# One stream of products with the values per pair of heads, single banks for their sums, and part of the result sums in retention

## The chip, the cores and the metric

The kernel runs on one core of a Trainium2 chip. The metric is the time of one execution on the device in microseconds (us): the median of several runs.

## The reference

The block takes x of 1024 positions by 1024 channels in float32. A modulated RMS norm gives h, and one projection of h gives the inputs of two token mixers that run side by side: retention with 4 heads, in chunks of 128 positions, and dilated sliding-window attention with three groups of 4 heads (window 128 with dilation 1, 512 with 4, 2048 with 16). Each group has its own softmax; the three are merged by their log denominators:

```python
for gi, (win, dil) in enumerate(ATT_GROUPS):
    o, lse = dilated_group(heads(aq), heads(ak), heads(av), tab, win, dil)   # softmax(q k + bias) v in the window
    outs.append(o); lses.append(lse)
wts = softmax(stack(lses, axis=0), axis=0)
att = einsum('gbhs,gbhsd->bshd', wts, stack(outs, axis=0)).reshape(B, S, ATT_GROUP_W)
att_out = att @ w_att_out
merged = sigmoid(gate_a) * ret_out + sigmoid(gate_b) * att_out
return merged @ w_o
```

A residual sum, a second norm, an MLP with a squared ReLU and a final norm follow. They are not touched here.

## The kernel before

Everything is float32, computed as three products of a high and a low part each (`mm3`, lines 200, 202 and 204: low weight by high input, high by low, high by high). The parts are made by a cast on ScalarE and a subtraction on VectorE.

The work is a list of steps (`Steps`, line 54). A step is one projection of h (`proj_gen`, which yields after each block of six matmuls) with other work woven between its matmuls. Weights come from DRAM into a ring of three raw tiles, and are split into their two parts ahead of the step that uses them: for an ordinary step before its body runs, for a step marked `manual` when its body calls `ahead`. Instructions are issued to each engine's queue in the order in which the Python code runs, and each engine works its queue in order; a tile's buffer is used again when its last reader is done.

PSUM has eight banks of 512 float32 columns. From the attention on they are dealt as two tiles of two banks (`ps_mm`, tag "mm", for projections and for the sums over the values) and four single banks (`ps_s`, tag "s", for scores and transpositions).

Retention (`chunk`, line 731) runs 4 heads of 8 chunks one after the other, and is called once per chunk. GpSimd has two operations in each chunk: `gr` (line 809), a power that VectorE needs for `nb` (line 715), and the subtraction `j` (line 639), the low part of q and k for a later chunk. Retention's output y goes to DRAM in four quadrants. `result_sums` (line 593), called at the start of attention, makes four sums of quadrants from DRAM to DRAM: eight DMAs of 2 MB on GpSimd's queue, four copies and four that add to their target. They are read much later as the inputs of the product with the output weights.

Attention runs in two pairs of heads; a pair has six combinations of group g and head a, in the order g = 1, 2, 0 (`combos`). Steps ak0 to ak5 project the keys and weave the scores in; `scores_end` leaves the probabilities in tiles P. `weights` (line 1571) turns the softmax statistics into the merging weights, which go through DRAM to be laid out for groups 1 and 2, and `pscale` (line 1600) multiplies the probabilities by them, half on VectorE (line 1605) and half on ScalarE (line 1607). Then come gate steps (`cover_step`), projections whose result goes through a sigmoid (line 1777) straight out of PSUM and to DRAM (line 1778). The products with the values are woven between their matmuls. In the first pair they are gate00 (n=0, with the last scores), gate01 (n=1), gate02 (n=2, with the products of group 0) and gate03 (n=3, group 1); group 2's products lie in ak0 of the second pair, named ak10. The second pair has gate04, gate05 and gate06 (group 0), and `gate_step` (gate9, groups 1 and 2).

One item of the products is a bank of up to four 128x128 transpositions of P (`pv_tr`, line 1622), a cast into the high part (`pth`, line 1626), a subtraction for the low part (`ptl`, line 1627), and later the products (`pv_mm`, lines 1646 to 1648) that add to a sum of 1024 columns in a two-bank tile. A pair has 20 items: four for each head of groups 0 and 1, two for each of group 2. Products run three items behind the transpositions; the queue of items is filled at the beginning of each call of `pv` and drained at its end. `pv_end` takes a finished sum out of PSUM into P of group 0: a copy for group 0 (line 1655), additions for groups 1 and 2 (line 1659), and at the end the split into `ah` and `al` (lines 1664, 1665). The values come by `v_fetch` (line 1529) and are split in `v_split` (lines 1539, 1540).

Of the kernel before, what the change touches and what calls it, by code (L numbers as in the profile page):

```python
# [11 lines left out]
F32 = mybir.dt.float32  # L12
# [5 lines left out]
P = 128  # L18
# [115 lines left out]
def block_kernel(ctx, tc, io, stop=None, dbg=None):  # L134
# [12 lines left out]
    def banks(single):  # L147

        if PS:
            PS["ctx"].close()  # L150
        PS["i"] = PS.get("i", 0) + 1
        PS["ctx"] = ExitStack()
        PS["p"] = PS["ctx"].enter_context(tc.tile_pool(name=f"psum{PS['i']}", bufs=2, space=bass.MemoryType.PSUM,
                                                       reuse_waits="tile"))
        PS["n"] = 8 if single else 4

    banks(True)

    def ps_mm(name):
        return PS["p"].tile([P, 2, 512], F32, tag="mm", bufs=2, name=name)  # L160

    def ps_s(name, shape=(P, 512)):
        return PS["p"].tile(list(shape), F32, tag="s", bufs=PS["n"], name=name)

# [416 lines left out]

    def dma_sum(out, x, y):

        flat = lambda t: t.rearrange("p a b -> p (a b)").rearrange("p (a b) -> p a b", b=2048)
        nc.gpsimd.dma_start(flat(out), flat(x))
        nc.gpsimd.dma_start(flat(out), flat(y), accum_op=ALU.add, max_dma_last_dim=8192)

# [4 lines left out]

    def result_sums():
        b11, b12, b21, b22 = (y_d[:, i] for i in range(4))
        dma_sum(yt_d["t1"], b11, b12)
        dma_sum(yt_d["t3"], b12, b22)
        dma_sum(yt_d["t2"], yt_d["t1"], b22)
        dma_sum(yt_d["t4"], yt_d["t2"], b21)

# [131 lines left out]
    def chunk(h, c, ahead, w=None):  # L731
# [6 lines left out]
        if g == 2:  # L738
            first["release"]()
        if w:  # L740
            hd["w"] = w
# [620 lines left out]

    A = {}
    att_ctx = ExitStack()
# [169 lines left out]

    def v_split(pair, g):
        for j in range(2):
            lo = A["l", g, j]
            hi = v_tile(pair, g, j, "vh")
            nc.scalar.copy(hi, fv(lo))
            nc.vector.tensor_sub(lo, fv(lo), fv(hi))  # L1540
            A["v", g, j] = (hi, lo)

# [20 lines left out]
    def stats_out(pair, g):  # L1563

        if g == 1:
            A["stn"] = A["p"].tile([P, 3, 8, 4], F32, tag="stn", name=f"stn{pair}")
        d = dram.tile([S, 4], F32, name=f"std{pair}{g}")
        nc.sync.dma_start(natural(d, g, 4), blocks(A["st"][:, g], g))
        nc.sync.dma_start(A["stn"][:, g], natural(d, 0, 4))

    def weights(pair):
# [10 lines left out]
        for g in range(3):  # L1582
            nc.vector.tensor_sub(wt[:, g], stn[g][:, :, 0:2], mx)
        nc.scalar.activation(wt, wt, AF.Exp)
        for g in range(3):
            nc.vector.tensor_mul(pr[:, g], wt[:, g], stn[g][:, :, 2:4])
# [9 lines left out]
        for g in (1, 2):  # L1596
            nc.sync.dma_start(blocks(wg[:, g - 1], g), natural(ds[g - 1], g, 2))
            A["w", g] = wg[:, g - 1]

    def pscale(g, a):  # L1600
        t, w = A["P", g, a], A["w", g]
        for blk in range(8):
            v = pslice(g, t, blk)[0]
            if blk in (0, 2, 4, 5, 7):
                nc.vector.tensor_scalar_mul(v, v, w[:, blk, a:a + 1])
            else:
                nc.scalar.mul(v, v, w[:, blk, a:a + 1])
        A["scaled", g, a] = True

# [19 lines left out]

    def pv_mm(g, a, bank, pt, acc, seen):  # L1630
        ph, pl = pt
# [7 lines left out]
        for i, q, k, n in runs:  # L1639
            cs = slice(i * 128, (i + n) * 128)  # L1640
            bk = q // 4
            o = acc[:, bk, (q % 4) * 128:(q % 4 + n) * 128]
            v = (vblk(g, k, a, 0), vblk(g, k, a, 1))
            first = bk not in seen
            seen.add(bk)
            nc.tensor.matmul(o, v[1], ph[:, cs], start=first, stop=False, skip_group_check=True)
            nc.tensor.matmul(o, v[0], pl[:, cs], start=False, stop=False, skip_group_check=True)
            nc.tensor.matmul(o, v[0], ph[:, cs], start=False, stop=True, skip_group_check=True)

    def pv_end(pair, g, a, acc):  # L1650

        f = flat(acc)
        sumt = A["P", 0, a][:, :1024]
        if g == 0:
            nc.scalar.copy(sumt, f)
        else:
            r = 4 * g
            sv = sumt.rearrange("p (i r) -> p r i", r=r)
            nc.vector.tensor_add(sv, f.rearrange("p (r i) -> p r i", r=r), sv)
        if g == 2:  # L1660
            h = 2 * pair + a
# [5 lines left out]

    def pv(pair, *groups):


        items = [(g, a, bank) for g in groups for a in range(2) for bank in PT[g]]
        accs = {}
        queue = []

        def mm(g, a, bank, pt):
            if (g, a) not in accs:
                accs[g, a] = (ps_mm(f"pv{pair}{g}{a}"), set())
            pv_mm(g, a, bank, pt, *accs[g, a])
            if bank is PT[g][-1]:
                pv_end(pair, g, a, accs[g, a][0])  # L1680
                return True
            return False

        for item in items:
            if item[2] is PT[item[0]][0]:
                del A["scaled", item[0], item[1]]
            queue.append((*item, pv_tr(pair, *item)))
            yield item is items[2]
            if len(queue) == 3:
                yield mm(*queue.pop(0))  # L1690
        for item in queue:
            yield mm(*item)

    def weave_pv(main, n, pair, *groups):


        parts, waits = sum(4 * len(PT[g]) for g in groups), 2 * len(groups) + 1
        heavy = max(1.0, (parts - waits) / max(1, n - waits))
        total = parts + waits * (heavy - 1)
        done = share = 0  # L1700
        for wait in pv(pair, *groups):
            share += heavy if wait else 1
            while done * total < share * n:
                next(main, None)
                done += 1
        drain(main)

    combos = [(g, a) for g in (1, 2, 0) for a in range(2)]

    def att_step(pair, i):  # L1710
# [3 lines left out]
        def body(*args):  # L1714
            ps = ps_mm(f"ak{pair}{i}")
            gen = proj_gen(ps, hd.pop("w") if i == pair == 0 else args[-1])
            if i == len(combos) - 1:
                v_fetch(pair, 0)
# [3 lines left out]
            elif pair == 0:  # L1722
# [6 lines left out]
                u_final(H - 1)  # L1729
                result_sums()  # L1730
                open_att()
                args[0](3)
            else:

                weave_pv(at(gen, 0, lambda: v_split(0, 2)), NK - 1, 0, 2)
# [3 lines left out]
            k_split(pair, g, a, ps)  # L1739
            if i > 0:  # L1740
# [5 lines left out]
    def cover_step(pair, n):  # L1746


        i = COVER[pair][n]

        def body(*args):
            ps = ps_mm(f"gate0{i}")
            gen = proj_gen(ps, args[-1])
            if n == 0:
                v_fetch(pair, 1)
                weave(gen, 6, scores_gen(pair, *combos[-1]), len(SB[0]), lag=2, rest=False)
                drain(gen)
                scores_end(pair, *combos[-1])
                weights(pair)
                for a in range(2):  # L1760
                    pscale(0, a)
            elif n == 1:
                drain(at(gen, 4, lambda: v_split(pair, 0)))
            elif n == 2:
                v_fetch(pair, 2)

                gen = at(gen, 3, lambda: (args[0](3), v_split(pair, 1)))
                weave_pv(gen, NK - 1, pair, 0)
                for a in range(2):
                    pscale(1, a)  # L1770
            else:
                weave_pv(at(gen, 3, lambda: [pscale(2, a) for a in range(2)]), NK - 1, pair, 1)
            if n > 1:
                t = A["r1"].tile([P, S], F32, tag="att", bufs=8, name=f"g0{i}s")
            else:
                t = ring(f"g0{i}s", F32)
            nc.scalar.activation(t, flat(ps), AF.Sigmoid)
            nc.sync.dma_start(gate_d[i], t)
        return body

    for pair in range(2):
        for i, (g, a) in enumerate(combos):
            steps.add(att_step(pair, i),
                      ([] if i == pair == 0 else [wsplit(io["w_ak"][g * 4 + 2 * pair + a])]) +
                      ([(aq_d[pair, *combos[i - 1]], q_prep(pair, *combos[i - 1]))] if i > 0 else []),
                      manual=i == pair == 0)
        for n in range(len(COVER[pair])):
            more = [(aq_d[pair, *combos[-1]], q_prep(pair, *combos[-1]))] if n == 0 else []
            steps.add(cover_step(pair, n), more + [wsplit(io["w_gate"][len(COVER[0]) * pair + n])], manual=n == 2)

# [4 lines left out]

    def gate_step(w):

        ps = ps_mm("gate9")
        gen = at(proj_gen(ps, w), 2, lambda: v_split(1, 2))
        gen = at(gen, 3, lambda: [pscale(2, a) for a in range(2)])  # L1800
        weave_pv(gen, NK - 1, 1, 1, 2)
        att_ctx.close()
# [12 lines left out]

    steps.add(gate_step, [wsplit(io["w_gate"][len(COVER[0] + COVER[1])])])

# [885 lines left out]
```

## Time and profile before

| | before |
|---|---|
| median of 3 runs | 2194.77 us (2193.68 to 2197.47) |
| the profiled execution's own time | 2196.09 us |
| its span in the trace | 2194.1 us |
| TensorE busy | 2151.7 us (98%) |
| VectorE busy | 1472.7 us (67%) |
| ScalarE busy | 944.5 us (43%) |
| GpSimd busy | 166.4 us (8%) |
| mean granted TensorE clock | 0.998 |

Engines are named PE (TensorE matmul), PEld (its weight loads), DVE (VectorE), ACT (ScalarE), POOL (GpSimd) and SP (the queue that issues most DMAs). A row of waits names the waiting engine, tile and line, then what it waited for and where that is written, then the total, the count and the longest in us. A row of a timeline has start and length in us, engine, line, operation, written and read tiles, and in brackets the idle time before it with its releaser. A row of groups has busy us and mean ns behind the bar, then the idle time before it. A tile's view has the minimum, median and maximum length in ns. The end of a matmul is modelled.

### The profile page before, as it was taken

The numbers are of one execution on the slowest core, as the hardware profiler recorded it, in microseconds if no ns is written. First come the engines' busy times: TensorE is split into PE (matmuls) and PEld (weight loads), VectorE is DVE, ScalarE is ACT, GpSimd is POOL, SyncE is SP. The second block draws the span as 40 slices with busy tenths as digits, with TensorE's granted clock in tenths as the row PEclk, the third lists the DMA queues.
The fourth block names the chain that finished last, engine by engine and source line by source line (L and its number), as shares of the span: only waits on it lengthen the run. The fifth ranks groups of instructions, "written<-read, shape, count | busy, mean of one in ns | idle before, by whom it ended". The sixth has DMA issues, their size and how long they took to land.

```text
span 2194.1 us, 26997 instructions
## 1 busy us (share of the span) xinstructions
PE 2151.7 (98%) x10034; PEld 1784.1 (81%) x10034; DVE 1472.7 (67%) x2271; ACT 944.5 (43%) x1709; POOL 166.4 (8%) x176
## 2 busy tenths in 40 slices
PE   7999999999999999999999999999999999999998
PEld 5888888888888888888788788888878888788887
DVE  6756777767566677755555644777876665787855
ACT  4532322333334566654544524434454544533412
POOL 0101111100001233200000000001000000000003
PEclk9999999999999999999999999999999999999999
DMA  9869999734687745579523364654154435645322
GB/s 382 227 199 293 289 308 279 222 130 149 244 294 291 250 159 192 173 239 258 151 78 107 106 240 170 234 187 139 44 206 149 152 137 193 243 135 175 113 86 78
DMA packets 159906, 422.54 MB, mean 193 GB/s; under 512 B 27478, under 2 KB 55389, under 8 KB 155358
## 3 DMA queue, kind: packets, MB, share of 16 engines
q1 hardware_dynamic: 151902, 372.57, 48.2%
q0 software_dynamic: 7872, 48.24, 9.5%
q8 instruction: 79, 1.29, 0.2%
q14 instruction: 53, 0.43, 0.1%
HBM read 325.71 MB, written 160.32 MB: 222 GB/s over the span
## 4 chain that ended last, share of the span: by engine, by line
PE 84%; DVE 7%; ACT 4%; DMA 3%; issue 1%; SPq 0%; POOL 0%; POOLq 0%; DVEq 0%; ACTq 0%
PE qap L200 6%; PE qap L204 6%; PE qap L202 6%; PE fp L200 4%; PE fp L202 4%; PE fp L204 4%; PE f2a L202 2%; PE f2a L204 2%; PE f2a L200 2%; PE ak L200 1%; PE ak L202 1%; PE ak L204 1%; PE rg L202 1%; PE rg L200 1%; PE rg L204 1%; PE va L204 1%
## 5 line engine op out<-in xcount | busy, mean ns | idle before, releaser
L200 PE MATMUL qap<-hh,qaw 128*128 128x512 f32 x264 | 102.9, 390 | 0.5 <-DVE qat L291 0.5
L204 PE MATMUL qap<-hh,qaw 128*128 128x512 f32 x264 | 102.7, 389 | 0.0
L202 PE MATMUL qap<-hl,qaw 128*128 128x512 f32 x264 | 102.7, 389 | 0.0
L639 POOL TENSOR_TENSOR j<-qk,j 128x512 fp32r<-128x512 f32 x32 | 48.1, 1506 | 324.1 <-ACT j L638 324.1
L2158 ACT ACTIVATE a<-a 128x512 f32<-128x512 f32 x48 | 30.3, 632 | 78.2 <-DVE a L2157 78.2
L2054 POOL TENSOR_TENSOR accnf<-accnf,sqnf 128x256 f32<-128x256 f32 (+1 forms) x18 | 16.6, 922 | 612.4 <-ACT sqnf L2053 612.4
L1510 ACT ACTIVATE P<-P,ng 128x128 f32<-128x128 f32 (+1 forms) x96 | 41.9, 438 | 43.9 <-DVE ng L1507 43.9
L200 PEld LDWEIGHTS qap<-hh,qaw 128*128 128x128 f32 x264 | 49.5, 188 | 11.5 <-DVE qat L291 1.4
L204 PEld LDWEIGHTS qap<-hh,qaw 128*128 128x128 f32 x264 | 49.6, 188 | 10.3
L202 PEld LDWEIGHTS qap<-hl,qaw 128*128 128x128 f32 x264 | 49.5, 188 | 10.3
L2347 ACT CAST w2h<-w2s 128x512 fp32r<-128x512 f32 x36 | 22.4, 621 | 78.4 <-DVE w2s L2385 78.4
L257 DVE TENSOR_TENSOR fw<-w1r,fw 128x512 fp32r<-128x512 f32 x48 | 32.8, 688 | 33.3 <-ACT fw L247 33.3
L257 DVE TENSOR_TENSOR qaw<-wa,qaw 128x512 fp32r<-128x512 f32 x66 | 45.0, 686 | 12.7 <-ACT qaw L247 12.6
L2054 POOL TENSOR_TENSOR accn<-accn,sqn 128x512 f32<-128x512 f32 x12 | 15.5, 1295 | 477.2 <-ACT sqn L2053 477.2
L247 ACT CAST qaw<-wa 128x512 fp32r<-128x512 f32 x66 | 39.8, 617 | 25.5 <-PE qap L204 15.3
L200 PE MATMUL fp<-h2h,fw 128*128 128x512 f32 x128 | 50.0, 391 | 0.0
L204 PE MATMUL fp<-h2h,fw 128*128 128x512 f32 x128 | 49.8, 389 | 0.0
L202 PE MATMUL fp<-h2l,fw 128*128 128x512 f32 x128 | 49.8, 389 | 0.0
L200 PE MATMUL roa<-rh,rwl 128*128 128x512 f32 x128 | 49.8, 389 | 0.0
L202 PE MATMUL roa<-rl,rwh 128*128 128x512 f32 x128 | 49.8, 389 | 0.0
L204 PE MATMUL roa<-rh,rwh 128*128 128x512 f32 x128 | 49.8, 389 | 0.0
L1288 DVE SCALAR_TENSOR_TENSOR cossin<-cossin,cb 128x1024 f32<-128x1024 f32 x32 | 39.0, 1219 | 15.9 <-DMA cossin<-in_w_ada_dram 15.9
(3057 smaller groups left out, 7106.1 us busy)
## 6 DMA issues: line engine op xcount, KB each, us to landing
cossin<-in_w_ada_dram SPq DMA_DIRECT2D x32, 512.0 KB, 5.4
v<-vd SPq DMA_DIRECT2D x32, 512.0 KB, 4.7
w1r<-in_w_ff_dram SPq DMA_DIRECT2D x32, 512.0 KB, 4.9
vd<-vo SPq DMA_DIRECT2D x24, 512.0 KB, 6.6
yt<-y POOLq DMA_DIRECT2D x6, 2048.0 KB, 15.3
xsd<-as SPq DMA_DIRECT2D x24, 512.0 KB, 3.0
w2r<-in_w_ff2s_dram SPq DMA_DIRECT2D x24, 512.0 KB, 7.4
em<-in_w_ada_dram SPq DMA_DIRECT2D x16, 512.0 KB, 10.2
```

The source lines that it names most:

```text
L200: nc.tensor.matmul(o, wl, xh, start=first, stop=False, skip_group_check=skip)
L202: nc.tensor.matmul(o, wh, xl, start=False, stop=False, skip_group_check=skip)
L204: nc.tensor.matmul(o, wh, xh, start=False, stop=last, skip_group_check=skip)
L247: nc.scalar.copy(t[:, :512], src)
L257: nc.vector.tensor_sub(t[:, 512:], src, fv(t[:, :512]))
L639: nc.gpsimd.tensor_sub(t[:, 1], src, fv(t[:, 0]))
L1288: nc.vector.scalar_tensor_tensor(t, t, 1.0, cb, op0=ALU.mult, op1=ALU.mult, accum_out=mods[:, j:j + 1])
L1510: nc.scalar.activation(v, v, AF.Exp, bias=ng[:, blk:blk + 1], accum_out=st[:, g, blk, 2 + a:3 + a])
L2054: (nc.vector if f == 7 else nc.gpsimd).tensor_add(G["acc", key], G["acc", key], sq)
L2158: nc.scalar.activation(o, o, AF.Relu)
L2347: nc.scalar.copy(hi, src)
```

## The change

1. The products with the values of a pair become one generator, `pv_stream`, of 40 parts (20 transposition items, 20 products). `weave_pv` runs a given number of parts in each step: 16 in gate02, 14 in gate03 and 10 in ak10 for the first pair, 20 in gate06 and 20 in gate9 for the second. A projection's first block comes after the first three parts of a pair, or after the first two in a later step. `pscale` of a head comes two items before its first transposition.
2. While a stream runs, PSUM is dealt anew (`banks_pv`): one two-bank tile for projections, two single banks for transpositions, and four single banks for the sums, one for each head and half. `pv_end` works by halves of 512 columns.
3. Gate n=0 is copied out of PSUM by ScalarE and gate n=1 by VectorE at the end of their steps; their sigmoids run at parts 3 and 5 of the stream (`gate_out`).
4. The values' split is divided: for group 0 the casts are made in step n=0 and the subtractions inside `weights`; for groups 1 and 2 they are made at parts 12, 15, 24 and 27 (`pv_calls`). The fetch for group 0 comes one step earlier.
5. The reads of statistics and merging weights from DRAM are put off to `later_loads`, and the steps with streams, with n=1 and the first of the second pair are manual, calling `ahead` at named parts.
6. The result sums of retention's heads 0 and 1 are made by 16 DMAs of 512 KB, one issued at the start of each chunk from the last of head 1 on. The eight at the start of attention, for heads 2 and 3, are of 1 MB.

```diff
+    def ps_ac(name, j):
+        tag = f"ac{j % 4}"
+        return PS["first"].pop(tag, None) or PS["p"].tile([P, 512], F32, tag=tag, bufs=1, name=name)
+    def banks_pv(order):
+        banks(False)
+        PS["n"], PS["mm"] = 2, 1
+        for t in order:
+            PS["first"][t] = ps_mm("mmf") if t == "mm" else ps_s("sf") if t == "s" else ps_ac(t + "f", int(t[2]))
...
+        if c == 7 and h in (1, 2):
+            hd["sums"] = result_sums(slice(2 * h - 2, 2 * h))
+        if hd.get("sums"):
+            hd["sums"].pop(0)()
...
-    def pv_end(pair, g, a, acc):
-        f = flat(acc)
+    def pv_end(pair, g, a, acc, hf):
         sumt = A["P", 0, a][:, :1024]
         if g == 0:
-            nc.scalar.copy(sumt, f)
+            nc.scalar.copy(sumt[:, 512 * hf:512 * hf + 512], acc)
         else:
-            r = 4 * g
-            sv = sumt.rearrange("p (i r) -> p r i", r=r)
-            nc.vector.tensor_add(sv, f.rearrange("p (r i) -> p r i", r=r), sv)
+            n = 2 * g
+            sv = sumt.rearrange("p (i r) -> p r i", r=2 * n)[:, n * hf:n * hf + n]
+            nc.vector.tensor_add(sv, acc.rearrange("p (r i) -> p r i", r=n), sv)
...
+        for k, (g, a, i) in enumerate(PV):
+            if k + 2 < len(PV) and PV[k + 2][2] == 0:
+                pscale(*PV[k + 2][:2])
+            queue.append((g, a, i, pv_tr(pair, g, a, PT[g][i])))
+            yield
             if len(queue) == 3:
-                yield mm(*queue.pop(0))
+                mm(*queue.pop(0))
+                yield
...
+    def weave_pv(main, n, pair, parts, ahead, last=None):
+        lead = 2 if first == 0 else 1
+        for y in range(parts):
+            next(A["pv", pair])
+            while done < n and done * (parts - lead - 1) <= (y - lead) * n:
                 next(main, None)
                 done += 1
+            for call in calls.get(first + y, ()):
+                call()
+    def pv_calls(pair):
+        calls = {1: [later_loads], 3: [lambda: gate_out(pair, 0)], 5: [lambda: gate_out(pair, 1)]}
+        for g, y in ((1, 12), (2, 24)):
+            for j in range(2):
+                calls[y + 3 * j] = [lambda g=g, j=j: v_split(pair, g, j)]
+        for y in (9, 20, 35) if pair == 0 else (9, 22):
+            calls[y] = [lambda: calls["ahead"](3)]
...
             if n == 0:
+                later_loads()
+                for j in range(2):
+                    vs_high(pair, 0, j)
+                t = ring(f"g0{i}s", F32)
+                nc.scalar.copy(t, flat(ps))
+                A["gate", 0] = t, t
                 scores_end(pair, *combos[-1])
                 weights(pair)
-                for a in range(2):
-                    pscale(0, a)
+                pscale(0, 0)
             elif n == 1:
-                drain(at(gen, 4, lambda: v_split(pair, 0)))
+                drain(gen)
+                t = ring(f"g0{i}s", F32)
+                nc.vector.tensor_copy(t, flat(ps))
+                A["gate", 1] = t, t
-            nc.scalar.activation(t, flat(ps), AF.Sigmoid)
-            nc.sync.dma_start(gate_d[i], t)
```

More of the change, by code (lines that the diff above doesn't have):

```diff
@@ L1628, in pv_tr, with pv_mm @@
         return ph, pl
-    def pv_mm(g, a, bank, pt, acc, seen):
+    def pv_mm(pair, g, a, bank, pt, accs):
         ph, pl = pt
@@ L1689, in pv @@
             if len(queue) == 3:
-                yield mm(*queue.pop(0))
+                mm(*queue.pop(0))
+                yield
         for item in queue:
[L1692 to L1703, printed above, removed]
+            mm(*item)
```

152 lines of the change are left out of this document (87 added, 65 removed).

## The prediction

> **What bounds the kernel now.** I read the page first, then busy time by stage around the changed code, then TensorE's waits in the two stages where the sums over the values run, then the timeline of one of those waits. The page:
>
> ```profile
> span 2194.1 us, 26997 instructions
> ...
> PE 2151.7 (98%) x10034; PEld 1784.1 (81%) x10034; DVE 1472.7 (67%) x2271; ACT 944.5 (43%) x1709; POOL 166.4 (8%) x176
> ...
> PE 84%; DVE 7%; ACT 4%; DMA 3%; issue 1%; SPq 0%; POOL 0%; POOLq 0%; DVEq 0%; ACTq 0%
> ```
>
> TensorE is busy for 2151.7 of 2194.1 us, so all idle time of it in the whole kernel is 42 us. The change leaves the count of TensorE's instructions as it is; it can only take idle time of that engine away, or add some. Where it is, by stage (columns: length, then busy time and count of each engine, TensorE's granted clock, DMA share, GB/s):
>
> ```profile
> core 0: us, PE busy (x) PEld busy (x) DVE busy (x) ACT busy (x) POOL busy (x), PEclk, DMA share, GB/s
> 720.00:943.00 223.00, 222.89 (x1130) 185.97 (x1129) 171.82 (x331) 145.26 (x344) 68.14 (x62) 1.00 0.57 186
> 943.00:1049.00 106.00, 105.07 (x534) 88.91 (x534) 54.77 (x84) 53.86 (x142) 6.90 (x8) 1.00 0.89 263
> 1049.00:1115.00 66.00, 60.11 (x366) 51.10 (x365) 38.09 (x57) 32.63 (x53) 0.00 (x0) 1.00 0.45 124
> 1115.00:1208.00 93.00, 93.00 (x480) 79.30 (x479) 47.74 (x78) 43.12 (x123) 0.00 (x0) 1.00 0.30 86
> 1208.00:1263.00 55.00, 50.00 (x323) 43.02 (x322) 35.63 (x54) 30.07 (x49) 0.00 (x0) 1.00 0.33 106
> ```
>
> The rows are retention, the first pair's scores, its products with the values, the second pair's scores, and its products. Retention and the second pair's scores leave TensorE nothing to gain (0.11 and 0.00 us idle); the first pair's scores leave 0.93. The two stages of products leave 5.89 and 5.00. The granted clock is 1.00 in all five. What ended the waits in the two stages (total, times, longest), first pair and then second:
>
> ```profile
> PE pv L1646 <- DVE P L1659: 1.7, 2, 0.9
> PE gate L200 <- ACT g00s L1777: 1.6, 1, 1.6
> PE pv L1647 <- DVE ptl010(0, 0, 0)_9136 L1627: 1.2, 1, 1.2
> PE pv L1646 <- DVE vl L1540: 0.7, 1, 0.7
> PE pv L1647 <- DVE ptl000(0, 0, 0)_8923 L1627: 0.5, 1, 0.5
> PE pv L1646 <- ACT pth000(0, 0, 0)_8922 L1626: 0.3, 1, 0.3
> ```
>
> ```profile
> PE pv L1646 <- DVE P L1659: 1.7, 2, 0.9
> PE pv L1647 <- DVE ptl110(0, 0, 0)_10475 L1627: 1.2, 1, 1.2
> PE gate L200 <- ACT g04s L1777: 0.8, 1, 0.8
> PE pv L1646 <- issue: 0.5, 1, 0.5
> PE pv L1647 <- DVE ptl100(0, 0, 0)_10262 L1627: 0.5, 1, 0.5
> PE pv L1646 <- ACT pth100(0, 0, 0)_10261 L1626: 0.3, 1, 0.3
> ```
>
> They sum to 6.0 and 5.0 us, which is the idle time of the two stages. There are three kinds: a matmul that waits for the bank pair that a sigmoid or the addition into P still reads; products that begin before the low part of their transposed probabilities is there, at each start of the stream; and late splits of the values.
>
> The waits are a little longer than these rows say, because a matmul's end is drawn later than the next one could start:
>
> ```profile
> 1049.09 1.28 ACT L1777 ACT_TABLE_LOAD   x1
> 1050.38 1.02 ACT L1777 ACTIVATE g00s<-gate 128x1024 f32<-128x1024 f32 x1
> ```
>
> ```profile
> 1049.27 0.60 PE L1622 MATMUL pt000(0, 0, 0)_8917<-ct,P 128*128 128x128 f32 x4
> 1051.46 0.73 PE L200 MATMUL gate<-hh,raw_8581l 128*128 128x512 f32 x2 [1.59 <-ACT g00s L1777]
> ...
> 1052.95 0.60 PE L1622 MATMUL pt000(2, 1, 2)_8932<-ct,P 128*128 128x128 f32 x4
> ...
> 1056.76 0.28 PE L1648 MATMUL pv<-pth000(0, 0, 0)_8922,vh 128*128 128x256 f32 x1
> 1056.88 0.28 PE L1646 MATMUL pv<-pth000(0, 0, 0)_8922,vl 128*128 128x256 f32 x1
> ```
>
> Matmuls drawn 0.28 long start 0.12 apart. Each wait is thus about 0.16 us longer from start to start. With seven waits in each stage (the 14 of the rows) the two stages hold 11.0 + 14 x 0.16 = 13.2 us that could go.
>
> **The sigmoid's wait.** The timeline shows the first: gate02 may start when g00s has been read out of its bank pair, and that activation stands behind the scaling of P and a table load, and ends at 1051.40. Now ScalarE copies gate n=0 out of PSUM at the end of its step and VectorE does it for n=1; the sigmoids follow at parts 3 and 5 of the stream, reading SBUF. The 1.6 and 0.8 go. The sigmoids and the table load stay on ScalarE, which is busy for 32.63 of 66 and 30.07 of 55 us. They hold back a cast (pth) by up to 2.3 us once; the products come two items later, so I take nothing for it.
>
> **The stream.** The change runs all 20 transpositions and 20 product parts of a pair as one stream with three items under way, so that the fill (0.5 + 0.3 and 1.2 in each stage) comes once per pair, not once per call. The values are cast on ScalarE in the step before (n=0) and the low parts taken inside the weights' computation, so the 0.7 (vl) and most of the 0.5 (issue) go.
>
> **Single banks.** A sum now has two banks of 512 columns of its own, four in all, so the next head's sum doesn't wait for the addition. The two additions of one pair that TensorE waited for (1.7 in each stage) go. The price is two banks for transpositions where there were four, and one bank pair for the projections where there were two. These durations decide whether that costs anything (a mean in ns stands behind the bar; L775 has min, median and max):
>
> ```profile
> L1626 ACT CAST pth000(0, 0, 0)_8922<-pt000(0, 0, 0)_8917 128x512 fp32r<-128x512 f32 x1 | 0.6, 582 | 0.0
> ```
>
> ```profile
> L1659 DVE TENSOR_TENSOR P<-pv,P 128x1024 f32<-128x1024 f32 x4 | 8.4, 2100 | 3.0 <-PE pv L1648 3.0
> L1540 DVE TENSOR_TENSOR vl<-vl,vh 128x1024 fp32r<-128x1024 f32 x6 | 7.1, 1219 | 0.3 <-ACT vh L1539 0.3
> ...
> L1627 DVE TENSOR_TENSOR ptl000(0, 0, 0)_8923<-pt000(0, 0, 0)_8917,pth000(0, 0, 0)_8922 128x512 fp32r<-128x512 f32 x1 | 0.7, 687 | 0.0
> ```
>
> ```profile
> L775 DVE COPY state<-kv x4: 1224/1225/1225, 726.6 to 889.5; 128x1024 f32<-128x1024 f32 x4
> ```
>
> A transposition's bank is free once the cast (0.58) and the subtraction (0.69) have read it, 1.27 us after it if both engines are idle. In the stream, the transposition that reuses the bank comes two items later. The first stage has 60 us of matmuls for 20 items, so two items are about 6 us; the second has 50, so 5 us. That covers 1.27 plus a split of 1.22 and a half-width addition (half of 2.10) ahead of it on VectorE. So in the middle of the stream I take nothing.
>
> At its start there is no cover: the first three transpositions stand one behind the other with no projection between them. Four are drawn 0.60 long in the row of 1049.27, 0.44 without the 0.16 of overhang, so the third wants its bank 0.9 us after the first began. VectorE first has the copy of gate n=1 to do: a copy of 128x1024 out of PSUM takes 1.22 (the L775 row). Then comes the first low part, 0.69. If the copy starts with the overhang of the last projection's matmul, 0.16 us in, the bank is free at 0.16 + 1.22 + 0.69 = 2.1. So TensorE stands for **about 1.2 us once per pair**, a wait that was not there before. From below it is 0.4 (if the subtraction went ahead of the copy: 0.58 + 0.69 - 0.9), from above 2.4 (if a split of 1.22 came before it too); I take 1.2, by the order in which VectorE's instructions are issued.
>
> With one bank pair for projections, gate03 can start when the sigmoid of gate02 (1.02 by the row of g00s) has read its pair; TensorE has the products and transpositions of an item, about 1 to 2 us, in between. By my count of the order it just fits in the first pair and misses by about 0.25 in the second. I take 0.3 in all; from above it is a sigmoid's 1.0 for each of three changes, 3.0.
>
> The split weights are prepared at named parts (9, 20, 35) and the reads of the statistics are issued later on SP's queue, behind fewer waits. Both have more than 10 us before their users; nothing taken.
>
> **Sum over the stages.** 13.2 - 2 x 1.2 - 0.3 = 10.5 us saved.
>
> **The result sums.** Sums for heads 0 and 1 (16 DMAs of 512 KB on GpSimd's queue) move into 16 of the last 17 chunks of retention, one each; the eight that stay at the start of attention halve from 2 MB. There TensorE has 0.93 us to give back at most, and it waits for VectorE in them, so I count 0. In retention each DMA stands in GpSimd's order between the power gr of one chunk and the subtraction j, and most must wait for the landing of the DMA before. What is known of these:
>
> ```profile
> 865.95 0.54 POOL L809 TENSOR_TENSOR gr<-gr,ct 128x1 f32<-128x1 f32 x1 [2.36 <-DVE gr L808]
> 869.07 1.30 POOL L639 TENSOR_TENSOR j<-qk,j 128x512 fp32r<-128x512 f32 x1 [2.58 <-ACT j L638]
> ```
>
> ```profile
> 870.23 0.15 DVE L715 SCALAR_TENSOR_TENSOR nb<-ba,gr 128x1 f32<-128x1 f32 x1
> ```
>
> ```profile
> L809 POOL TENSOR_TENSOR gr<-gr,ct x8: 542/643/1597, 845.3 to 893.1; 128x1 f32<-128x1 f32 x8
> ```
>
> ```profile
> L573 POOL DMA_DIRECT2D wros<-in_w_ret_out_dram x16: 772/860/1349, 302.5 to 423.6; - x16
> ...
> DMA to landing us min/median/max: 3.4/7.8/16.7
> ```
>
> GpSimd is idle for 223.00 - 68.14 = 155 us of 32 chunks, 4.8 us in a chunk of 7.0. An issue takes 0.86 by its row for sums of the weights, which fits. What waits behind a late DMA is j (needed a chunk later) and the next gr; nb on VectorE needs that only 3.7 us after its end (866.49 to 870.23), and GpSimd had stood for 2.4 before it. So about 6 us of lag costs nothing. Landing at the median of 7.8 (the weights' sums, of the same size) lags 0.8 in a chunk; three dependent DMAs in a row make 2.4. So 0, from the 6 us.
>
> **Rivals.**
> *All waits go.* If the low part goes ahead of the gate's copy, and gate03 starts in time, 13.2 less 0.8 is saved: 2183.7 on the profiled run, 2182.4 on the median. Against it stands the order on VectorE.
>
> *Half of it comes back.* The one bank pair costs 3.0, and the first low part 2.4 per pair: 13.2 - 3.0 - 4.8 = 5.4 us saved, 2189.4 on the median.
>
> *Two transposition banks make TensorE wait throughout* (slower). VectorE is busy for 35.63 us of the second stage; in 50.5 us that would be 71%. Where the scaling of P for the next group, a split (1.22) and an addition of two halves come together ahead of a low part, its 0.69 can end 5 us after the transposition, which is all the cover. It decides from 10.5 / 40 = 0.26 us per item on; at 0.6 us for each of 40 items it is 24 - 10.5 = +13.5, 2208.3. For it speaks that two banks leave no slack for uneven load; against it, that VectorE has over a quarter of the stage free.
>
> *The sums slow retention* (slower). If a landing takes L, three dependent ones lag 3 x (L - 7.0); what exceeds 6 us delays every later chunk. That starts at L = 9 and eats up the whole gain at 2 x (3 x (L - 7.0) - 6) = 10.5, L = 10.8; at L = 13 it is 24 us, again 2208.3. What speaks for it is the maximum of 16.7 and VectorE's load of 171.82 of 223 us beside it, with GpSimd's gr stretched from 0.54 to 1.60 at times. Against it are the median of 7.8 and a DMA share of 0.57. A rule of the Trainium skill speaks for this rival (SBUF — State Buffer, section "SBUF: two separate sides"): descriptors of a DMA on GpSimd's queue are written by GpSimd, which is locked out while VectorE runs a two-port operation, and a transfer of about 620 ns then takes about 3100. The spread of gr's row fits such a lock; whether it reaches these DMAs no run here shows. If each landing grew by that 2.5 us from the median of 7.8, the estimate by that page is L = 10.3: 2 x (3 x 3.3 - 6) = 7.8 us, and 2.7 of the gain would be left.
>
> **How the numbers follow.** The profiled run took 2196.09 us, 2.0 more than its span and 1.3 more than the median of 2194.77. Less 10.5 the profiled run is 2185.6, and the median **2184.3 us**. A comparison can tell about 0.2%, 4.4 us, from no change. Chances: the forecast (6 to 12 us saved) 0.52; all waits gone 0.12; half of it back 0.13, of which 0.03 within 4.4 us; nothing gained, the two prices cancelling, 0.05; banks 0.10, of which 0.01 is within 4.4; retention 0.08, of which 0.01 within. Faster 0.74, same 0.10, slower 0.16. The range runs from 2179 (the first rival, 0.93 of the scores, and 2% of the 110 us of busy matmuls, should small gaps inside them close too) to 2197; it leaves out most of the two slower cases (0.14) and a tail of the first rival (0.03). The likeliest case alone is 2182 to 2189.
>
> **What would show it.** Right: the waits for L1659, for g00s and g04s and for vl are gone; each stage has one wait of about 1.2 us for ptl000 and ptl100 at the third transposition; the stages shorten by about 5.5 and 4.5 us; retention, from the first chunk to the last, keeps its length within 1 us. Wrong: waits of transpositions for ptl all through the stages, a wait of gate03 or gate9 for a sigmoid of over 1 us, or idle TensorE in the last 17 chunks of retention with nb late on VectorE.

## The result and the profile after

The changed kernel takes 2183.84 us (median of 4 runs, 2182.82 to 2185.33) against 2195.01 us for the kernel before (4 runs, 2193.68 to 2197.47): a ratio of 0.9948, with a 95% interval from 0.9931 to 0.9966. The profiled execution took 2182.82 us, 13.3 less than the one before. The page of the changed kernel, in the lines shown of the one before:

```profile
span 2181.1 us, 27045 instructions
...
PE 2147.4 (98%) x10034; PEld 1784.6 (82%) x10034; DVE 1479.0 (68%) x2281; ACT 947.1 (43%) x1715; POOL 178.4 (8%) x192
...
PE 90%; DVE 4%; ACT 2%; DMA 1%; issue 1%; POOL 0%; SPq 0%; POOLq 0%; DVEq 0%; ACTq 0%
```

TensorE's share of the chain that ended last rose from 84% to 90%. Busy time by stage, cut at the same points of the work as before (retention, scores, products, scores, products):

```profile
core 0: us, PE busy (x) PEld busy (x) DVE busy (x) ACT busy (x) POOL busy (x), PEclk, DMA share, GB/s
720.00:942.00 222.00, 221.89 (x1127) 185.16 (x1126) 173.51 (x331) 144.71 (x342) 81.71 (x78) 1.00 0.73 223
942.00:1047.70 105.70, 105.14 (x536) 89.19 (x535) 56.02 (x82) 55.23 (x142) 5.47 (x8) 1.00 0.69 201
1047.70:1106.80 59.10, 58.06 (x365) 51.08 (x363) 36.80 (x62) 32.45 (x54) 0.00 (x0) 1.00 0.35 101
1106.80:1200.60 93.80, 93.80 (x486) 79.97 (x485) 51.04 (x78) 44.64 (x122) 0.00 (x0) 1.00 0.31 91
1200.60:1248.50 47.90, 46.86 (x316) 41.99 (x315) 33.42 (x60) 28.16 (x50) 0.00 (x0) 1.00 0.35 105
```

From TensorE's first transposition of a pair to its first matmul behind the stage, the first stage of products went from 65.8 to 59.1 us, the second from 54.0 to 48.1. The first pair's scores went from 106.7 to 106.1. Retention kept its 220.9 us (221.0 before), though the sums raised its DMA share from 0.57 to 0.73. These are 6.7 + 5.9 + 0.6 = 13.2 us; the other stages moved by under 1 us. TensorE's waits in the five stages, now three in all:

```profile
PE sc L221 <- DVE kl L1478: 0.6, 1, 0.6
```

```profile
PE pt000(4, 1, 4)_8951 L1653 <- DVE ptl000(0, 0, 0)_8929 L1658: 1.0, 1, 1.0
```

```profile
PE pt100(4, 1, 4)_10312 L1653 <- DVE ptl100(0, 0, 0)_10290 L1658: 1.0, 1, 1.0
```

The two new ones are the predicted wait of the third transposition. Its timeline (start, length) on VectorE, ScalarE and TensorE:

```profile
1047.96 1.23 DVE L1836 COPY g01s<-gate 128x1024 f32<-128x1024 f32 x1 [2.38 <-PE gate L223]
1049.10 0.68 DVE L1658 TENSOR_TENSOR ptl000(0, 0, 0)_8929<-sf,pth000(0, 0, 0)_8928 128x512 fp32r<-128x512 f32 x1
```

```profile
1048.39 0.58 ACT L1657 CAST pth000(0, 0, 0)_8928<-sf 128x512 fp32r<-128x512 f32 x1 [2.83 <-PE sf L1653]
```

```profile
1047.76 0.60 PE L1653 MATMUL sf<-ct,P 128*128 128x128 f32 x4
1048.19 0.60 PE L1653 MATMUL pt000(2, 1, 2)_8932<-ct,P 128*128 128x128 f32 x4
1049.84 0.66 PE L1653 MATMUL pt000(4, 1, 4)_8951<-ct,P 128*128 128x128 f32 x4 [1.04 <-DVE ptl000(0, 0, 0)_8929 L1658]
```

The third group begins 1.65 us after the second, where 0.44 would do: 1.2 us. But the cast ends at 1048.97, and the low part begins at 1049.10, so without VectorE's copy it would have begun only about 0.1 us earlier. The wait is that of a transposition, a cast and a subtraction in a row, with no projection between the transpositions.

### The profile page after: what moved, and what is told of

Same layout as the page of the kernel before. It is cut to its first block, busy times and chain, and to the rows that moved or that the text cites. A ratio compares the mean times of both kernels' runs of the same rounds, so it can differ in the third digit from the quotient of the medians.

```text
span 2181.1 us, 27045 instructions
## 1 busy us (share of the span) xinstructions
PE 2147.4 (98%) x10034; PEld 1784.6 (82%) x10034; DVE 1479.0 (68%) x2281; ACT 947.1 (43%) x1715; POOL 178.4 (8%) x192
## 3 DMA queue, kind: packets, MB, share of 16 engines
q1 hardware_dynamic: 151902, 372.57, 48.4%
## 4 chain that ended last, share of the span: by engine, by line
PE 90%; DVE 4%; ACT 2%; DMA 1%; issue 1%; POOL 0%; SPq 0%; POOLq 0%; DVEq 0%; ACTq 0%
PE qap L219 6%; PE qap L223 6%; PE qap L221 6%; PE fp L219 4%; PE fp L223 4%; PE fp L221 4%; PE ak L219 2%; PE ak L221 2%; PE ak L223 2%; PE f2a L221 2%; PE f2a L223 2%; PE f2a L219 2%; PE rg L221 1%; PE rg L219 1%; PE rg L223 1%; PE va L221 1%
## 5 line engine op out<-in xcount | busy, mean ns | idle before, releaser
L656 POOL TENSOR_TENSOR j<-qk,j 128x512 fp32r<-128x512 f32 x32 | 48.3, 1513 | 311.7 <-ACT j L655 311.7
L276 DVE TENSOR_TENSOR qaw<-wa,qaw 128x512 fp32r<-128x512 f32 x66 | 45.0, 686 | 11.1 <-ACT qaw L266 11.1
L1955 DVE TENSOR_TENSOR rwl<-rwl,rwh 128x1024 fp32r<-128x1024 f32 x25 | 30.2, 1221 | 29.0 <-ACT rwh L1985 29.0
L221 PE MATMUL fp<-h2l,fw 128*128 128x512 f32 x128 | 49.8, 389 | 0.0
L223 PE MATMUL fp<-h2h,fw 128*128 128x512 f32 x128 | 49.8, 389 | 0.0
L219 PE MATMUL roa<-rh,rwl 128*128 128x512 f32 x128 | 49.8, 389 | 0.0
L221 PE MATMUL roa<-rl,rwh 128*128 128x512 f32 x128 | 49.8, 389 | 0.0
L223 PE MATMUL roa<-rh,rwh 128*128 128x512 f32 x128 | 49.8, 389 | 0.0
## 6 DMA issues: line engine op xcount, KB each, us to landing
wrvs<-in_w_rv_dram POOLq DMA_DIRECT2D x16, 512.0 KB, 11.1
```

The lines of the kernel that those rows point to most:

```text
L219: nc.tensor.matmul(o, wl, xh, start=first, stop=False, skip_group_check=skip)
L221: nc.tensor.matmul(o, wh, xl, start=False, stop=False, skip_group_check=skip)
L223: nc.tensor.matmul(o, wh, xh, start=False, stop=last, skip_group_check=skip)
L276: nc.vector.tensor_sub(t[:, 512:], src, fv(t[:, :512]))
L656: nc.gpsimd.tensor_sub(t[:, 1], src, fv(t[:, 0]))
```

## Experiments

All times of stages below are measured in the trace, from the first transposition of the pair to the first matmul behind its products and their projections. An experiment without such a change has 59.1 and 48.1 in every run, within 0.02, so 0.2 us can be told there. The total of one run can't tell 2 us.

**The sums back at the start of attention.**

```diff
-        if c == 7 and h in (1, 2):
-            hd["sums"] = result_sums(slice(2 * h - 2, 2 * h))
-        if hd.get("sums"):
-            hd["sums"].pop(0)()
...
-                for add in result_sums(slice(4, 8)):
+                for add in result_sums(slice(0, 8)):
```

> The changed kernel with all result sums back at the start of attention (eight DMAs of 2 MB). Theory (the gain is TensorE's waits in the two stages of products, the move of the sums is worth nothing): the first pair's products take 59.1 us and the second's 48.1 us as in the changed kernel (65.8 and 54.0 before), the first pair's scores 106 to 107 us, retention 221 us; the time stays within 2 us of the changed kernel's 2183.8. Rival (the sums held up the early attention, and their move is part of the gain): 3 to 6 us slower, with new waits of TensorE between the last chunk and the end of gate01.

Measured: 2187.38 us in one run; stages of 65.9 and 48.1, scores 106.2, retention 220.9. Both theories were wrong: the early attention doesn't care, but the whole gain of the first stage is gone. What waited, for TensorE, VectorE and ScalarE, and the issues of the queue SP (start, length):

```profile
PE pt010(0, 0, 0)_9095 L1649 <- DVE ptl001(4, 1, 4)_9053 L1654: 4.4, 1, 4.4
```

```profile
DVE P L1633 <- DMA wg<-wtd: 5.7, 1, 5.7
```

```profile
ACT P L1635 <- DMA wg<-wtd: 7.0, 1, 7.0
```

```profile
1045.21 1.01 SPq L1623 DMA_DIRECT2D wtd<-wt  x2
1046.32 13.47 SPq L1550 DMA_DIRECT2D vl<-vad  x2
1063.96 1.87 SPq L1595 DMA_DIRECT2D wg<-wtd  x2
```

The tile view of the merging weights in DRAM (wtd, two stores and two reads) gives the landings that the trace holds; the shortest is a read's and the longest a store's:

```profile
DMA to landing us min/median/max: 3.9/11.3/18.7
```

The store of 8 KB was issued at 1045.21 and landed 18.7 us later, while the last DMA of 2 MB, issued at 1043.8, was under way. Only then could the weights be read back, at 1063.96. The two issues of `vl` in between took 13.47 us on SP's queue, 1.08 in the changed kernel, but they were over at 1059.8, so it is the store that decided. The stream wants to scale group 1 with them about 1062, two items ahead; ScalarE and VectorE stood in order behind that scaling for 7.0 and 5.7 us, and with them the low part that TensorE needed. In the changed kernel the same read is issued 14.5 us earlier:

```profile
1049.44 5.32 SPq L1599 DMA_DIRECT2D wg<-wtd  x2
```

In the kernel before the store took 17.2 us as well, but the scaling of group 1 began only at 1069.0, so nobody waited:

```profile
DMA to landing us min/median/max: 17.2/17.2/17.2
```

```profile
L1605 DVE TENSOR_SCALAR P<-P,wg x20: 278/281/346, 1069.0 to 1084.7; 128x128 f32<-128x128 f32 x16, 128x256 f32<-128x256 f32 x4
```

The wait of 4.4 us is not all of the 6.8 us lost. The rest is TensorE's granted clock behind it (more at the end):

```profile
1073.00:1077.00 4.00, 4.00 (x18) 3.52 (x18) 2.15 (x3) 2.21 (x4) 0.00 (x0) 0.57 0.00 0
```

**The moved sums alone, on the kernel before.** The edit is part 6 of the change and nothing else.

> The kernel before with only the result sums changed as in the changed kernel (heads 0 and 1 in retention, heads 2 and 3 at the start of attention). With the sums all at the start, the changed kernel's first stage of products took 65.9 us and waited 7.0 us for the merging weights, whose 8 KB store landed after 18.7 us. Theory (the sums' traffic only hurts a kernel that asks for the merging weights early; the one before asks at 1069 us, when they are there): first stage 65.0 to 65.9 us (65.8 before), second 54.0; the first pair's scores 0.5 us shorter. Rival (the traffic by itself costs the stage some us, the stream nothing): first stage 59 to 62 us.

Measured: 2194.12 us in one run; the first stage 65.0 us, the second 54.0, the scores 0.6 shorter. That is the theory. The store now landed after 4.6 us, not 17.2, and nobody had waited for it. Of the waits in the first stage one has changed, from 1.6:

```profile
PE gate L200 <- ACT g00s L1780: 0.8, 1, 0.8
```

Without the sums beside the scores ScalarE gets to the sigmoid 0.8 us earlier against TensorE's work (its table load starts 1.0 us ahead of the first transposition, 0.2 before). What had held it up was a load: in the kernel before ScalarE waited 1.7 us for q (`raw<-aqd`) at 1019.5, here not at all, and the scores' work on VectorE and ScalarE stands 0.8 us earlier from there on. So in the first stage the sums alone bring 0.8, the stream without them nothing, both together 6.7.

**Twice the sums' traffic in retention.**

```diff
+    scr = [dram.tile([P, 2, 512], F32, name=f"scr{k}") for k in range(4)]
...
+            k = hd["nx"] = hd.get("nx", -1) + 1
+            nc.gpsimd.dma_start(scr[k % 4].rearrange("p a b -> p (a b)"), y_d[:, 0, 0:2].rearrange("p a b -> p (a b)"))
             hd["sums"].pop(0)()
```

> The changed kernel; ahead of each of the 16 DMAs of sums in retention another copy of 512 KB to a scratch tensor is issued on the same queue. Theory of the prediction's price (most DMAs wait on GpSimd for the landing of the one before, three in a row may lag by 6 us): with a landing of 7.0 us now and 10 to 13 then, 2 x (3 x (L - 7.0) - 6) gives 6 to 24 us more in retention (221 us now), and TensorE idle in its second half. Rival (these waits are hidden altogether, since j is made a chunk ahead): retention stays within 1 us of 221 us.

Measured: 2188.56 us in one run; retention 227.6 us, 6.7 more, the rest unchanged. GpSimd's wait for landings, TensorE's two longest waits, and the stages in retention's second half:

```profile
POOL yt L605 <- DMA yt<-y: 14.1, 4, 6.5
```

```profile
PE oT L706 <- DVE kl L686: 3.2, 2, 2.6
...
PE sT L668 <- POOL j L657: 0.7, 1, 0.7
```

```profile
840.00:900.00 60.00, 58.41 (x296) 48.06 (x296) 47.98 (x86) 38.83 (x92) 28.84 (x34) 1.00 1.00 321
900.00:942.00 42.00, 39.35 (x191) 32.48 (x190) 31.30 (x57) 25.93 (x59) 18.20 (x20) 0.96 0.93 266
```

The 6.7 us lie in the theory's range, but they don't come by its way, and they aren't hidden as the other theory has it. GpSimd does wait for landings, and j comes late behind them, but that costs TensorE only 0.7 us. The longest wait, 2.65 us up to 911.26, comes from another queue: a load of q and k (`qk<-qkd`), issued by SP at 889.21, landed after 19.05 us; ScalarE stood for it for 4.1 us, and `kh`, `kl` and the transposition `oT` came late one after the other. These loads landed after 7.9, 11.6 and 19.1 us here (minimum, median, maximum), after 5.1, 7.5 and 11.6 in the changed kernel. TensorE's waits sum to 4.2 us, 4.9 from start to start; 1.7 more is its granted clock, which was 0.50 from 912.4 to 915.8 (0.96 in the row).

The formula looked at GpSimd's queue alone: with landings of its sums of 5.9, 8.2 and 11.1 us it gives nothing at the median and 2 x (3 x 4.1 - 6) = 12.6 at the maximum. In the changed kernel they are 4.9, 6.9 and 9.3, the median just inside the 7.0 us of a chunk.

**The sigmoids straight out of PSUM.**

```diff
-        calls = {1: [later_loads], 3: [lambda: gate_out(pair, 0)], 5: [lambda: gate_out(pair, 1)]}
+        calls = {1: [later_loads]}
...
-                nc.scalar.copy(t, flat(ps))
-                A["gate", 0] = t, t
...
                 pscale(0, 0)
+                t = ring(f"g0{i}s", F32)
+                nc.scalar.activation(t, flat(ps), AF.Sigmoid)
+                nc.sync.dma_start(gate_d[i], t)
...
-                nc.vector.tensor_copy(t, flat(ps))
-                A["gate", 1] = t, t
+                nc.scalar.activation(t, flat(ps), AF.Sigmoid)
+                nc.sync.dma_start(gate_d[i], t)
```

> The changed kernel with the sigmoids of gates n=0 and n=1 straight out of PSUM at the end of their steps as before, without the copies. By the prediction's term the early copies save 1.6 us in the first pair and 0.8 in the second, so these come back as waits of gate02 and gate06 for g00s and g04s: stages of 60.7 and 48.9 us or more. Rival (with only one head's probabilities scaled ahead of the sigmoid, and three items ahead of the projection, the bank pair is free in time): no such wait; instead the cast pth000 stands behind the second sigmoid (1.02 us) and the third transposition waits about 0.4 us longer, so 59.5 and 48.5 us.

Measured: 2184.43 us in one run; 59.5 and 48.5. The rival holds: no wait for g00s or g04s, and the third transposition waits 0.4 longer in each stage.

```profile
PE pt000(4, 1, 4)_8953 L1653 <- DVE ptl000(0, 0, 0)_8931 L1658: 1.4, 1, 1.4
```

**Both heads scaled at once; also with the sigmoids straight out of PSUM.**

```diff
-            if k + 2 < len(PV) and PV[k + 2][2] == 0:
-                pscale(*PV[k + 2][:2])
+            if k + 2 < len(PV) and PV[k + 2][1:] == (0, 0):
+                for x in range(2):
+                    pscale(PV[k + 2][0], x)
...
-                pscale(0, 0)
+                for x in range(2):
+                    pscale(0, x)
```

> The changed kernel with the probabilities of both heads of a group scaled at once, two items ahead of the first (for group 0 at the end of gate00), not one head at a time: ten scalings of 0.28 us on VectorE in a row, not five. Theory (two items give 5 to 6 us of cover in the stream, the cast, the low part and ten scalings take 1.3 + 2.8): stages within 0.3 us of 59.1 and 48.1. Rival (the spread of the scaling is what took away the waits for ptl010 and ptl110): these come back, 1.2 to 1.5 us in each stage.

Measured: 59.1 and 48.3. Scaling both heads at once costs nothing by itself.

> The changed kernel with both heads scaled at once and the first two sigmoids straight out of PSUM: at the boundary this is the order of the kernel before (scaling, table load, sigmoid), in the changed banks. Direct sigmoids alone gave 59.5 and 48.5. By the prediction's reading of the boundary gate02 and gate06 wait for g00s and g04s: 1.75 and 0.95 us from start to start come back. Rival (the merging weights are worked out 2 us earlier now, since their statistics aren't held up by the sums' traffic, so that the sigmoid is done ahead of the projection's first block even so): within 0.4 us of 59.5; in the second pair, which has no sums beside it, within 0.4 us of 48.5 too.

Measured: 62.2 and 49.8; neither theory. There is no wait for the sigmoids, but they and their table load now end at 1051.39, ahead of the first cast, and the wait of the third transposition is 2.5 us in both stages:

```profile
PE pt000(4, 1, 4)_8953 L1653 <- DVE ptl000(0, 0, 0)_8939 L1658: 2.5, 1, 2.5
```

```profile
PE pt100(4, 1, 4)_10312 L1653 <- DVE ptl100(0, 0, 0)_10298 L1658: 2.5, 1, 2.5
```

So the two edits, worth 0.4 and 0 to 0.2 us when undone singly, are worth 1.65 us in the second stage and 3.1 in the first together (the first with 1.7 us of a sunken clock, below). Each leaves ScalarE free in time without the other.

**Two banks for the sums.**

```diff
-        tag = f"ac{j % 4}"
+        tag = f"ac{j % 2}"
...
```

> The changed kernel with two single banks for the sums, one for each half, which both heads use in turn (two banks stand empty). By the prediction's term the extra banks save the two waits for P (L1659) of each stage, so they come back: 1.7 us and more in each stage, 61 and 50 us. Rival (working by halves is what matters: a half of the next sum begins two items after the same half of the last one ended, about 5 us, and its addition takes about 1.05 us): stages within 0.3 us of 59.1 and 48.1.

Measured: 59.1 and 49.9. Among the products there is no wait at all; the 1.7 us of the second stage stand behind its last product, where the next projection takes a bank that the last addition still reads:

```profile
PE ao L219 <- DVE P L1690: 1.6, 1, 1.6
```

Working by halves is thus what took away the waits for P; four banks, not two, matter only where the banks are dealt anew after the second stage.

**The queue drained at each group, alone and with both heads scaled at once.**

```diff
+            if k + 1 < len(PV) and PV[k + 1][0] != g:
+                while queue:
+                    mm(*queue.pop(0))
+                    yield
```

> The changed kernel with the queue of items drained at the end of each group, as the separate calls did before, so that each pair has three fills, not one. By the prediction's term a fill costs 1.2 to 2.0 us, so two more in each pair give 61.5 to 63 and 50.5 to 52 us. Rival (what cost time at a fill was other work ahead on VectorE; with projections between the transpositions a fill is covered): stages within 0.5 us of 59.1 and 48.1.

Measured: 61.3 and 48.9. The fill itself makes one wait of 0.5 us, in the second stage, which is 0.8 longer. In the first it is the single bank pair of the projections that costs 1.9: the drain moves parts so that too little lies between gate02 and gate03.

```profile
PE gate L219 <- ACT g02s L1845: 1.9, 1, 1.9
```

> Both heads scaled at once, and the queue of items drained at the end of each group: the order of the kernel before, in the banks of the changed one. Drained alone the stages took 61.3 and 48.9 us. Theory (a fill costs only where other work stands ahead of it on VectorE): with the scaling two items ahead the fill itself still finds VectorE free, 61.3 to 62 and 48.9 to 49.6. Rival (fill and piled scaling together were the wait for ptl010 of 1.4 us from start to start): 62.7 and 50.3 or more.

Measured: 63.3 and 48.4. The same wait of 1.9, no wait for a fill. Of the 2.0 us that the first stage lost beyond 61.3, 1.7 is the clock again; without it the stage lies in the theory's range, and the second lies below it. The rival is not borne out: draining and piling up don't bring the wait for ptl010 back in these banks, and which part of the order before made it is left open.

**The first projection block one transposition earlier.**

```diff
-        lead = 2 if first == 0 else 1
+        lead = 1
```

> The changed kernel with the projection's first block after the second transposition of a pair, not after the third (lead = 1 throughout). Theory (the wait of 1.0 us for ptl000 and ptl100, 1.2 us from start to start, is the transposition, cast and subtraction of an item without cover): a block of six matmuls is 1.37 us and covers it; each stage gets 1.1 to 1.3 us shorter (58.0 and 46.9), the whole 2.2 to 2.5 us. Rival (VectorE's copy of the gate, ahead of the first low part, sets the time, as the prediction has it, and the next wait only moves to the products): the stages get shorter by less than 0.5 us, and a wait for ptl000 stands ahead of the first product.

Measured: 2182.26 us in one run; 57.9 and 46.7, and in the five stages only the wait for kl is left. The theory holds.

> The first projection block one transposition earlier, and the first two sigmoids straight out of PSUM. The earlier block alone gave 57.9 and 46.7, without a wait. Theory (the block covers the 1.4 us that the third transposition waits with direct sigmoids, and the early copies are then worth nothing): within 0.3 us of these. Rival (the block now comes before the sigmoid has read its bank pair): a wait of gate02 or gate06 for g00s or g04s of 0.5 to 1.5 us.

Measured: 58.1 and 47.0, no wait for a sigmoid: with the earlier block, the early copies are worth 0.2 to 0.3 us in each stage.

> The kernel with the first projection block one transposition earlier again, timed. Its profile had stages of 57.9 and 46.7 us (59.1 and 48.1 in the changed kernel), 2.6 us less together. If this holds in the median: 2195.0 - 11.2 - 2.6 = 2181.2 us; if the rest of the kernel gives it back, 2183.8.

Measured: 2180.64 us (6 runs, 2179.8 to 2184.91) against 2196.18 (11 runs of the kernel before): a ratio of 0.9932, from 0.9919 to 0.9945. Its trace has the same 57.9 and 46.7, without idle time on TensorE:

```profile
1047.70:1105.60 57.90, 57.90 (x360) 50.87 (x359) 35.97 (x62) 31.45 (x53) 0.00 (x0) 1.00 0.34 99
1199.10:1246.00 46.90, 46.90 (x314) 42.15 (x313) 32.22 (x59) 28.08 (x50) 0.00 (x0) 1.00 0.35 100
```

## Why the prediction was right, and where its steps were not

The forecast of 2184.3 us is 0.5 from the median of 2183.84. The waits that it named are gone, one new wait of the size it named stands in each stage, and retention kept its length. That it is as near as 0.5 us is in part luck. The sum over the stages was 10.5 us and measured 13.2, and the profiled run took 2182.82 us where 2185.6 was forecast; the medians lie 11.2 apart, since the profiled run before was 1.1 above its median and the one after 1.0 below. The two stages were to shorten by 5.5 and 4.5 us and did so by 6.7 and 5.9. By its steps:

- *The waits that could go, 13.2 us.* All went. The two stages got 6.7 and 5.9 us shorter with two new waits of 1.2 in them, so 15.0 us went, 1.8 more than the sum of the 14 waits with their overhang of 0.16. I undersized these terms by that much. The range had allowed 2.2 us for small gaps among the matmuls; that the 1.8 is these is not shown.
- *The new wait, 1.2 us a pair.* It measured 1.2 in both. Its place is right, its cause only in part: I put it down to the copy ahead of the low part, and the copy delays it by about 0.1 us. The test with the earlier block shows that what lacked was cover.
- *One bank pair for projections, 0.3.* It measured 0. The test with the drained queue shows how near it is: 1.9 us for gate03 with a slightly different order.
- *The sigmoid's wait, 1.6 + 0.8.* It went, but not because of the copies. Undone alone they cost 0.4 a stage, as a longer wait elsewhere. The bank pair is free in time without them. In the first pair the sigmoid out of PSUM ended 2.1 us after the first transposition began in the kernel before, and 1.4 us with both heads scaled ahead of it and 0.1 us with one in the changed banks; the scaling starts 0.8 us earlier against TensorE. The three transpositions that now come before the projection (one before) take 1.3 us. So with one head scaled the pair is free, and with two it just about is.
- *Single banks, 1.7 a stage.* The waits for P went; two banks with halves do the same among the products.
- *The result sums, 0.* This step failed. I asked only whether TensorE waited for them in the early attention of the kernel before. The change itself asks for the merging weights some 7 us earlier, and the traffic of the sums would have held these up: 6.8 us. The more than 10 us that I gave the reads before their users turned into a wait of 7.0 us. The zero came out right since in the change the two come together; that is luck, not a term that I had worked out.
- *Retention, 0.* Right, by a margin that is thinner than I had it. The landing measured 6.9 us (7.8 foreseen). With twice the traffic it measured 8.2, and retention lost 6.7 us where the formula gave nothing, mostly by loads on SP's queue and the clock, which neither my sum nor its rival had. The rival drawn from the Trainium skill (SBUF — State Buffer, section "SBUF: two separate sides") didn't come about: issues on GpSimd's queue took 0.86 and 0.61 us beside VectorE's work in retention, and the landings (median 6.9 us) were no longer than the weights' earlier ones (7.8).

The banks rival didn't come about either: in the middle of the streams no transposition waited for its bank.

## What to carry to other kernels

When a change asks for data earlier, price its DMA chain at the new time, with what else is then on the queues: a store of 8 KB took 18.7 us beside transfers of 2 MB (4.6 and 5.1 without them), and a whole stage's gain hung on it. A wait named in the trace of before names who came last, not what the edit is worth: undone singly, the early copies and the scaling of one head at a time cost 0 to 0.4 us a stage, and together 1.65. Where a pipeline starts, put a block of independent matmuls between its first steps; here one line did it for 1.2 to 1.4 us a stage.

## What the runs showed of the hardware that was not expected

After some waits of TensorE the granted clock fell to 0.50, for 3.41 us or for 6.83 us. These are rows behind waits of 2.5 us (both heads scaled and direct sigmoids, first stage; the second row is a part of the first) and 1.9 us (drained and scaled at once):

```profile
1053.00:1057.00 4.00, 4.00 (x17) 3.44 (x16) 0.88 (x2) 0.59 (x1) 0.00 (x0) 0.57 0.98 260
```

```profile
1053.10:1056.30 3.20, 3.20 (x11) 2.65 (x10) 0.78 (x2) 0.59 (x1) 0.00 (x0) 0.50 0.93 247
```

```profile
1073.00:1077.00 4.00, 3.92 (x15) 3.34 (x16) 1.73 (x4) 1.26 (x4) 0.00 (x0) 0.59 0.33 131
```

Half the clock for 3.41 us costs a stage 1.7 us beyond the wait. The row of the sums at the start, above, is from a stretch of 6.83 us (1069.6 to 1076.4), of which TensorE worked 4.8: some 2.4 us. But after the same wait of 2.5 us in the second stage, and of 1.9 in the drained queue alone, the clock stayed at 1.00:

```profile
1208.30:1212.30 4.00, 3.98 (x29) 3.72 (x30) 1.62 (x3) 1.30 (x3) 0.00 (x0) 1.00 0.92 246
```

```profile
1073.30:1077.30 4.00, 3.98 (x22) 3.38 (x23) 2.99 (x9) 2.29 (x6) 0.00 (x0) 1.00 0.33 131
```

One wait is in all 14 traces of this case: 3.3 us in the MLP, near 1600 us. About its end the clock was 0.50 for 3.41 us in six of them (the kernels before and after among these), for 6.83 us in three and not at all in five. That alone moves a run by up to 3 us: the two runs of the earlier block took 2182.26 us with 6.83 us of it and 2179.8 with none.

The Trainium skill (TensorE: Matmul & The Clock Gate, section "What's actually happening") has the clock halved after an idle window of about 3.4 us whose phase is free-running. That a phase decides fits the mixed outcome; that waits of 1.9 and 2.5 us are enough is more than its sentence says, and the measurement decides.
